# A two-layer diffusion backbone: gate build on one engine, reordered candidate pairs, and early expert blocks in the routing

## The chip, the cores and the metric

The kernel runs on one core of a Trainium2 chip. A core has a matrix engine (TensorE, PE in the profile), a vector engine (VectorE, DVE), a scalar engine (ScalarE, ACT), a general one (GpSimd, POOL) and SyncE (SP), whose queue issues most transfers. Each engine runs its own instructions in their order and waits for others by semaphores. The metric is the device time of one execution in microseconds (us); lower is better.

## What is computed

Two layers over 512 latent tokens and 256 context tokens, 1024 wide. The part of a layer that matters here is its second half, a product-key expert network with 16384 experts:

```python
def _peer(xn, wq, sub_keys, u_tab, v_tab):
    s1, i1 = lax.top_k(s[:, :, 0], 16)          # s: 8 heads, two halves, 128 keys each
    s2, i2 = lax.top_k(s[:, :, 1], 16)
    cand_s = s1[..., :, None] + s2[..., None, :]
    cand_i = i1[..., :, None] * 128 + i2[..., None, :]
    top_s, pos = lax.top_k(cand_s, 16)          # over the 256 pairs
    idx, gate = take(cand_i, pos), softmax(top_s)
    a = gelu(einsum('nd,nhkd->nhk', xb, u_tab[idx])) * gate
    return einsum('nhk,nhkd->nd', a, v_tab[idx])
```

Layer 0 does this for all 768 tokens, layer 1 for the 512 latent ones. All data are float32.

## The kernel before

**Dense and gathered tokens.** For most latent tokens (`DENSE`: 512 in layer 0, 384 in layer 1) the experts are not gathered. Their gates are spread into a matrix G (16384 experts by tokens, mostly zeros), and the network is computed densely, in 128 blocks of 128 experts: `h = gelu(U_c x)`, times G, times `V_c`. The 256 context tokens of layer 0 and the last 128 latent tokens of layer 1 are gathered row by row from a table that holds u and v side by side: a generator (`gather`, L1208) that at every step fetches two table rows of 8 KB for each of 128 tokens (2 MB in all, issued from GpSimd's queue, L1249), and for the rows of earlier steps takes the dot product with x (L1231) and adds the weighted v (L1223), all of that on VectorE. A block of tokens takes 64 steps and three more.

**Stages of the second half**, in this order, with layer 0's place in the profiled execution:

- routing (`route`, L1050; 788 to 1009 us): 16 half-heads. For each, ScalarE and GpSimd split a weight block into a high and a low part (L1075, L1076), TensorE makes the queries with 24 matmuls and the key scores with 4, and VectorE picks the top 16 of 128 for each of four token tiles (L1107 to L1116). After every second head `route_pick` (L1132) runs for each tile as a generator of three pieces: GpSimd adds the pairs of sums and of ids into `rcd` (`CAND`: of the 256 pairs only 50 can hold one of the best 16); VectorE finds the best 8 and the next 8 (L1160 to L1168) and compares their places with an iota (L1172), GpSimd multiplies the one-hot result by the ids (`roh`, L1174); VectorE sums it (L1177).
- gate build (`build_g`, L1308; 1009 to 1295 us): 64 iterations of 8 tokens in layer 0, 48 in layer 1. In each, VectorE makes two one-hot tiles of 128x1024 float16 (`goa`, `gob`, L1353, L1354) and multiplies the first by the gates' high part (`go1`, L1355); the product with the low part (`go2`, L1359) is made by GpSimd, in every third iteration by VectorE. TensorE multiplies them (16 matmuls), ScalarE moves the result to a stage of 2 MB, and every four iterations SyncE writes that to memory (`Gd`).
- dense stage (`dense`, L1396; 1317 to 2615 us): 128 blocks, each with a hidden part (24 matmuls, L1383) and an output part (24 matmuls in layer 0, 18 in layer 1).

**Work put into other stages.** The hidden part of the blocks in `EARLY` (26 of each layer's 128) is computed ahead by the generator `early` (L1389) and written to memory, from where the dense stage loads it. Its split into a low part (`dul`, L1378) is GpSimd's; in the dense stage it is VectorE's. `advance(n)` takes n blocks from that generator: `ROUTE` per half-head (0), `TAIL` (8) behind the routing, 0.2 per iteration of the build, the rest behind the build. Likewise `steps(n)` takes n steps from the gathers: `STEP_BUILD` (0.15 and 0.1) per iteration of the build; what is left is spread evenly over the dense stage (L1470).

**What sets the order.** The program text is not the order on the engines: a scheduler places each instruction where its own model finds it ready, so that a few early blocks of `TAIL` stand between the routing's matmuls. The resulting order on each engine is fixed when the kernel is built.

## Time and profile before

| what | us |
|---|---|
| median of 3 runs | 4478.73 (4469.4 to 4480.89) |
| the profiled execution, its own time | 4476.18 |
| its span, first to last instruction | 4474.4 |
| TensorE busy in it | 3992.0 (89%) |
| VectorE busy | 3283.9 (73%) |
| GpSimd busy | 1705.1 (38%) |
| ScalarE busy | 1571.2 (35%) |

The page gives such shares for the whole span, in which stages with different limits follow each other. So the stretches of the stages have to be read apart: for each, the busy time of every engine, the clock that TensorE was granted as a part of full speed, and the busy share of the 16 transfer engines. A matmul's duration overlaps the next one's; how long one takes in a row of them is read from the distance between starts. The same holds for VectorE, by some 0.07 us.

### The profile page before, as it was taken

How to read it: one execution, taken by the hardware profiler on the slowest of the kernel's cores; microseconds unless marked ns; L12 is line 12 of the kernel's file. 1: busy time of each engine (PE TensorE's matmuls, PEld its weight loads, DVE VectorE, ACT ScalarE, POOL GpSimd, SP SyncE). 2: the span in 40 equal slices, each digit the busy share in tenths (PEclk: the TensorE clock that was granted, in tenths of full speed). 3: DMA queues.
4: the chain of work that ended last, by engine and by line, in shares of the span. 5: the costliest groups of instructions: out<-in, count | busy, mean ns of one | idle time of the engine just before them, and what ended most of it. 6: DMA issues, size and time to landing. Idle time of an engine off the chain costs nothing. (4 is left out here: it accounts for less than half of the span.)

```text
span 4474.4 us, 57073 instructions
## 1 busy us (share of the span) xinstructions
PE 3992.0 (89%) x20829; PEld 3352.4 (75%) x20829; DVE 3283.9 (73%) x6347; ACT 1571.2 (35%) x2562; POOL 1705.1 (38%) x1363
## 2 busy tenths in 40 slices
PE   7889878877869999999999969888868899999998
PEld 4568657666658888777888859677667799999998
DVE  2444686589978888788888755674889577777775
ACT  2332243325543333223323233433246333333332
POOL 2133354785633333233333133345876222222220
PEclk8899889988879999999999989989978899999999
DMA  7663221317779889888889634123257788788875
GB/s 264 226 208 108 60 71 62 112 61 221 227 250 352 332 333 335 322 319 324 338 334 343 247 114 119 50 81 100 65 164 216 265 307 303 294 311 301 301 300 168
DMA packets 429346, 996.46 MB, mean 223 GB/s; under 512 B 31448, under 2 KB 264280, under 8 KB 375816
## 3 DMA queue, kind: packets, MB, share of 16 engines
q1 hardware_dynamic: 372760, 586.46, 38.3%
q0 software_dynamic: 56304, 406.35, 24.4%
q8 instruction: 164, 2.69, 0.2%
q14 instruction: 118, 0.97, 0.1%
HBM read 909.97 MB, written 81.17 MB: 222 GB/s over the span
## 5 line engine op out<-in xcount | busy, mean ns | idle before, releaser
L1249 POOL DMA_INDIRECT uv<-in_peer_uv_dram,ridx x384 | 633.3, 1649 | 1558.2 <-DVE eacc L1223 1506.8
L141 PE MATMUL o<-dvh,dch 128*128 128x512 f32 x1792 | 702.0, 392 | 3.5 <-DVE do L1425 3.5
L141 PE MATMUL o<-dvl,dch 128*128 128x512 f32 x1792 | 701.3, 391 | 0.0
L141 PE MATMUL o<-dvh,dcl 128*128 128x512 f32 x1792 | 697.2, 389 | 0.0
L1383 PE MATMUL h<-xh,duh 128*128 128x512 f32 (+1 forms) x1632 | 602.9, 369 | 47.5 <-ACT duh L1377 39.9
L1383 PE MATMUL h<-xh,dul 128*128 128x512 f32 (+1 forms) x1632 | 604.8, 371 | 0.4 <-DVE dul L1378 0.3
L1383 PE MATMUL h<-xl,duh 128*128 128x512 f32 (+1 forms) x1632 | 602.2, 369 | 0.0
L1223 DVE SCALAR_TENSOR_TENSOR eacc<-uv,egf,eacc 128x1024 f32<-128x1024 f32 x381 | 492.4, 1293 | 0.0
L1231 DVE SCALAR_TENSOR_TENSOR uv<-uv,xn 128x1024 f32<-128x1024 f32 x384 | 470.3, 1225 | 0.0
L1377 ACT CAST duh<-du 128x1024 fp32r<-128x1024 f32 x256 | 268.7, 1050 | 535.4 <-PE h L1383 455.6
L1378 DVE TENSOR_TENSOR dul<-du,duh 128x1024 fp32r<-128x1024 f32 x204 | 249.5, 1224 | 261.9 <-ACT duh L1377 225.6
L141 PEld LDWEIGHTS o<-dvh,dch 128*128 128x128 f32 x1792 | 336.3, 188 | 78.1 <-DVE do L1425 7.2
L141 PEld LDWEIGHTS o<-dvh,dcl 128*128 128x128 f32 x1792 | 336.5, 188 | 73.6 <-DVE dcl L1462 0.3
L141 PEld LDWEIGHTS o<-dvl,dch 128*128 128x128 f32 x1792 | 336.3, 188 | 66.6
L1450 ACT CAST dvh<-dv 128x1024 fp32r<-128x1024 f32 x256 | 263.1, 1051 | 350.1 <-PE o L141 298.0
L1451 DVE TENSOR_TENSOR dvl<-dv,dvh 128x1024 fp32r<-128x1024 f32 x256 | 308.8, 1221 | 101.5 <-ACT dvh L1450 82.1
L1383 PEld LDWEIGHTS h<-xh,duh 128*128 128x128 f32 x1632 | 309.1, 189 | 90.2 <-ACT duh L1377 40.5
L1383 PEld LDWEIGHTS h<-xl,duh 128*128 128x128 f32 x1632 | 309.0, 189 | 42.1
L1383 PEld LDWEIGHTS h<-xh,dul 128*128 128x128 f32 x1632 | 308.6, 189 | 39.1 <-DVE dul L1378 1.9
L141 PE MATMUL mm<-go,gob 128*128 128x128 f16 x1792 | 238.1, 297 | 94.0 <-DVE go L1355 79.0
L141 PEld LDWEIGHTS <-gob 128*128 128x128 f16 x1792 | 194.8, 120 | 141.4 <-DVE go L1355 100.6
L1365 ACT ACTIVATE gst<-mm 128x512 f32<-128x512 f32 x224 | 226.3, 1120 | 166.3 <-PE mm L141 153.6
(352 smaller groups left out, 8027.9 us busy)
## 6 DMA issues: line engine op xcount, KB each, us to landing
du<-in_peer_ut_dram SPq DMA_DIRECT2D x256, 512.0 KB
dv<-in_peer_v_dram SPq DMA_DIRECT2D x256, 512.0 KB
Gd<-gst SPq DMA_DIRECT2D x28, 2048.0 KB
wa<-in_w_ada_dram SPq DMA_DIRECT2D x24, 2048.0 KB
w<-in_w_in_dram SPq DMA_DIRECT2D x78, 512.0 KB
dG<-Gd SPq DMA_DIRECT2D x32, 1024.0 KB
w<-in_peer_wq_dram SPq DMA_DIRECT2D x48, 512.0 KB
dG<-Gd SPq DMA_DIRECT2D x32, 768.0 KB
```

Source lines behind the costliest of these rows:

```text
L141: self.nc.tensor.matmul(out, lhsT=lhsT, rhs=rhs, start=start, stop=stop)
L1223: nc.vector.scalar_tensor_tensor(acc, t[:, D:], w, acc, op0=OP.mult, op1=OP.add)
L1231: nc.vector.scalar_tensor_tensor(t[:, :D], t[:, :D], 1.0, xn, op0=OP.mult, op1=OP.mult, accum_out=dots[:, k:k + 1])
L1249: nc.gpsimd.indirect_dma_start(t, None, a["peer_uv"], bass.IndirectOffsetOnAxis(ap=idx[:, k:k + 1], axis=0))
L1365: nc.scalar.activation(stage[:, :, q * 8 + g * 4:q * 8 + g * 4 + 4].rearrange("p i t -> p t i"), gp.rearrange("p (t i) -> p t i", i=P), AF ...
L1377: nc.scalar.copy(uh, u)
L1378: eng.tensor_sub(ul, u, uh.bitcast(F32))
L1383: nc.tensor.matmul(hp[:, :nd], lhsT=lt[:, k], rhs=rt[:, k, :nd], start=n == 0, stop=n == 3 * KD - 1)
L1450: nc.scalar.copy(vh, v)
L1451: nc.vector.tensor_sub(vl, v, vh.bitcast(F32))
```

## The change

Six things, all in the second half of the layers:

1. In the gate build the product `go2` is VectorE's in every iteration.
2. No gather steps are taken in the build (`steps(STEP_BUILD[l])` is gone); all of them fall to the dense stage.
3. While the build runs, the low part of an early block is made by VectorE instead of GpSimd.
4. `EARLY` has 32 blocks instead of 26, and `ROUTE` is 0.75: 12 blocks are taken within the routing, then 8 behind it and 0.2 per iteration of the build as before.
5. The 50 candidate pairs are reordered so that the 20 that can hold one of the best 8 come first. The first `max` and its `max_index` search those 20. The pairs are added by 12 GpSimd instructions per tile instead of 8.
6. The comparison, the product and the sum that turn places into ids work on 8 picks of 20 and 8 picks of 50 instead of 16 of 50, all three on VectorE and in the generator's third piece.

```diff
-STEP_BUILD = (0.15, 0.1)
-ROUTE = (0, 0)
+ROUTE = (0.75, 0.75)
-EARLY = (tuple(range(1, 128, 5)), tuple(range(1, 128, 5)))
+EARLY = (tuple(range(1, 128, 4)), tuple(range(1, 128, 4)))
-CAND = ((0, 1, 16, 0), (1, 1, 8, 16), (2, 1, 5, 24), (3, 1, 4, 29), (4, 1, 3, 33), (5, 3, 2, 36), (8, 8, 1, 42))
+CAND = ((0, 1, 0, 8, 0), (1, 1, 0, 4, 8), (2, 2, 0, 2, 12), (4, 4, 0, 1, 16),
+        (0, 1, 8, 8, 20), (1, 1, 4, 4, 28), (2, 1, 2, 3, 32), (3, 1, 2, 2, 35), (4, 1, 1, 2, 37), (5, 3, 1, 1, 39),
+        (8, 8, 0, 1, 42))
+NTOP = 20
...
-                    nc.vector.max(v0, ca[:, h])
+                    nc.vector.max(v0, ca[:, h, :NTOP])
...
-        eq = T(pw, [P, NCAND, K], F16, tag="req")
-        nc.vector.tensor_tensor(eq, tf[:, None, :].to_broadcast([P, NCAND, K]), iota, op=OP.is_equal)
-        oh = T(pw, [P, RH, 16, NCAND], tag="roh", bufs=nt // 2)
-        nc.gpsimd.tensor_mul(oh, eq.rearrange("p c (h k) -> p h k c", k=16),
-                             ci[:, :, None, :].to_broadcast([P, RH, 16, NCAND]))
         yield
-        nc.vector.tensor_reduce(ef[:, h0 * 16:(h0 + RH) * 16], oh.rearrange("p h k c -> p (h k) c"), axis=AX.X, op=OP.add)
+        for x, nx in enumerate((NTOP, NCAND)):
+            eq = T(pw, [P, nx, RH * 8], F16, tag=f"req{x}")
+            nc.vector.tensor_tensor(eq, tf[:, x].rearrange("p h k -> p (h k)")[:, None, :].to_broadcast([P, nx, RH * 8]),
+                                    iota[:, :nx], op=OP.is_equal)
+            oh = T(pw, [P, RH, 8, nx], tag=f"roh{x}")
+            nc.vector.tensor_mul(oh, eq.rearrange("p c (h k) -> p h k c", k=8),
+                                 ci[:, :, None, :nx].to_broadcast([P, RH, 8, nx]))
+            nc.vector.tensor_reduce(e4[:, :, x], oh, axis=AX.X, op=OP.add)
...
-                n += 1
+                nc.vector.tensor_tensor(o2, oa, bc(e16[3]), op=OP.mult)
                 self.advance(0.2)
-                self.steps(STEP_BUILD[l])
-                (nc.vector if n % 3 == 0 else nc.gpsimd).tensor_tensor(o2, oa, bc(e16[3]), op=OP.mult)
...
-            ge = self.hidden(l, c, pool, pool, xh, xl, "sm", self.nc.gpsimd)
+            ge = self.hidden(l, c, pool, pool, xh, xl, "sm", self.nc.vector if self.building else self.nc.gpsimd)
```

The order on the engines moves with it. On VectorE in layer 0's gate build, before (`go` stands for both products; L1359 is `go2`, here the third iteration's, and `uv`, `eacc` are a gather's):

```order
L1353 TENSOR_TENSOR goa_9524<-e_1789_8623,iota_1788_8621 128x1024
L1354 TENSOR_TENSOR gob_9525<-e_1790_8624,iota_1788_8621 128x1024
L1355 TENSOR_TENSOR go_2001_9526<-goa_9524,e_1791_8625 128x1024
L1359 TENSOR_TENSOR go_2002_9527<-goa_9524,e_1792_8626 128x1024
L1353 TENSOR_TENSOR goa_9554<-e_1789_8623,iota_1788_8621 128x1024
L1354 TENSOR_TENSOR gob_9555<-e_1790_8624,iota_1788_8621 128x1024
L1355 TENSOR_TENSOR go_2008_9556<-goa_9554,e_1791_8625 128x1024
L1223 SCALAR_TENSOR_TENSOR eacc_8864<-uv_9080,egf_9320,eacc_8864 128x1024
L1231 SCALAR_TENSOR_TENSOR uv_9323,dots_8863<-uv_9323,xn_4947 128x1024
L1231 SCALAR_TENSOR_TENSOR uv_9325,dots_8863<-uv_9325,xn_4947 128x1024
L1353 TENSOR_TENSOR goa_9627<-e_1789_8623,iota_1788_8621 128x1024
```

The same place after the change (L1362 to L1365 are the four operations of an iteration, L1385 is `dul`):

```order
L1362 TENSOR_TENSOR goa_10164<-e_1909_9259,iota_1908_9257 128x1024
L1363 TENSOR_TENSOR gob_10165<-e_1910_9260,iota_1908_9257 128x1024
L1364 TENSOR_TENSOR go_2118_10166<-goa_10164,e_1911_9261 128x1024
L1365 TENSOR_TENSOR go_2119_10167<-goa_10164,e_1912_9262 128x1024
L1385 TENSOR_TENSOR dul_10175<-du_10172,duh_10174 128x1024
L1362 TENSOR_TENSOR goa_10226<-e_1909_9259,iota_1908_9257 128x1024
L1363 TENSOR_TENSOR gob_10227<-e_1910_9260,iota_1908_9257 128x1024
L1364 TENSOR_TENSOR go_2129_10228<-goa_10226,e_1911_9261 128x1024
L1365 TENSOR_TENSOR go_2130_10229<-goa_10226,e_1912_9262 128x1024
```

The gather's rows are gone from the build, every iteration has four VectorE operations, and an early block's subtraction comes now and then. On TensorE, 12 early blocks stand in layer 0's build (15 before) and 11 in layer 1's (12 before).

On TensorE in layer 0's routing, before: the last two matmuls of an early block (`sm`) that stand behind a half-head's queries, the half-head's key scores, and the next half-head's queries:

```order
L1383 MATMUL sm_8477<-xh_6640,duh_8473 128x512
L1383 MATMUL sm_8477<-xl_6641,duh_8473 128x512
L141 MATMUL mm_7583<-keysT_7487,qt_7581 128x128 x4
L141 MATMUL mm_7619<-xh_6640,wh_7552 128x512
L141 MATMUL mm_7619<-xl_6641,wh_7552 128x512
L141 MATMUL mm_7619<-xh_6640,wl_7553 128x512
```

and after:

```order
L1390 MATMUL sm_7963<-xh_6724,duh_7959 128x512
L145 MATMUL mm_7921<-keysT_7791,qt_7919 128x128 x4
L1390 MATMUL sm_7963<-xl_6725,duh_7959 128x512
L1390 MATMUL sm_7963<-xh_6724,dul_7960 128x512
...
L1390 MATMUL sm_7963<-xl_6725,duh_7959 128x512
L1390 MATMUL sm_7963<-xh_6724,dul_7960 128x512
L145 MATMUL mm_7991<-xh_6724,wh_7856 128x512
L145 MATMUL mm_7991<-xl_6725,wh_7856 128x512
```

Before, 7 matmuls of an early block stand between a half-head's queries and its scores, and none behind the scores. After, 17 more of them stand behind the scores; so it is in six of the half-heads, and in four others 8 or 10. Counted over layer 0's routing, 20 early blocks stand ahead of the build instead of 11, and 7.8 of them (188 matmuls) behind the last key scores instead of 4.8 (116 matmuls); in layer 1 it is 19.1 instead of 13.8 blocks, and 162 instead of 146 matmuls behind the last scores.

On GpSimd in layer 0's routing, before (`wl` is a weight block's low part, `dul` an early block's, `roh` the product with the ids):

```order
L1149 TENSOR_TENSOR rcd_7770<-rsf_1486_6812 128x2x6
L1146 TENSOR_TENSOR rcd_7770<-rsf_1486_6812 128x4x8
L1076 TENSOR_TENSOR wl_7921<-w_7918,wh_7920 128x1024
L1174 TENSOR_TENSOR roh_8157<-req_8155,rcd_7737 128x1600
L1174 TENSOR_TENSOR roh_8175<-req_8173,rcd_7748 128x1600
L1076 TENSOR_TENSOR wl_7984<-w_7981,wh_7983 128x1024
L1174 TENSOR_TENSOR roh_8193<-req_8191,rcd_7759 128x1600
L1378 TENSOR_TENSOR dul_8576<-du_8573,duh_8575 128x1024
L1174 TENSOR_TENSOR roh_8211<-req_8209,rcd_7770 128x1600
```

and after:

```order
L1151 TENSOR_TENSOR rcd_7722<-rsf_1514_6896 128x4x3
L1151 TENSOR_TENSOR rcd_7722<-rsf_1514_6896 128x4x8
L1080 TENSOR_TENSOR wl_7857<-w_7854,wh_7856 128x1024
L1385 TENSOR_TENSOR dul_8055<-du_8052,duh_8054 128x1024
L1080 TENSOR_TENSOR wl_7954<-w_7951,wh_7953 128x1024
L1385 TENSOR_TENSOR dul_8369<-du_8366,duh_8368 128x1024
L1080 TENSOR_TENSOR wl_8049<-w_8046,wh_8048 128x1024
```

The products with the ids are gone; the subtractions of weights and of early blocks take turns.

## Rows read from the trace of the kernel before

**Rows 1.** From the page: busy time, share of the span and instructions of each engine.

```profile
PE 3992.0 (89%) x20829; PEld 3352.4 (75%) x20829; DVE 3283.9 (73%) x6347; ACT 1571.2 (35%) x2562; POOL 1705.1 (38%) x1363
```

**Rows 2.** Stretches: us, busy PE, PEld, DVE, ACT, POOL, clock, transfer share, GB/s.

```profile
788.00:1009.00 221.00, 181.09 (x777) 143.76 (x777) 161.33 (x826) 65.73 (x130) 173.21 (x177) 0.91 0.27 84
1009.00:1317.00 308.00, 226.83 (x1395) 182.61 (x1395) 273.38 (x292) 157.03 (x185) 171.29 (x79) 0.84 0.71 228
1317.00:2615.00 1298.00, 1283.41 (x5520) 1039.87 (x5520) 1090.60 (x1465) 386.10 (x578) 394.71 (x246) 0.99 0.84 317
3060.00:3285.00 225.00, 182.84 (x863) 157.59 (x864) 162.94 (x833) 72.69 (x143) 180.89 (x183) 0.90 0.29 89
3285.00:3501.00 216.00, 159.78 (x1070) 140.67 (x1069) 189.99 (x191) 117.36 (x138) 121.77 (x54) 0.83 0.69 216
3501.00:4474.40 973.40, 961.29 (x4750) 866.87 (x4750) 702.17 (x928) 350.20 (x519) 199.55 (x121) 0.99 0.77 285
```

**Rows 3.** Timeline of VectorE in layer 0's build: start, us, what.

```profile
1226.42 0.68 DVE L1359 TENSOR_TENSOR go<-goa,e 128x1024 f16<-128x1024 f16 x1
1227.02 0.68 DVE L1354 TENSOR_TENSOR gob<-e,iota 128x1024 f16<-128x1024 f16 x1
...
1228.23 2.88 DVE L1353 TENSOR_TENSOR goa<-e,iota 128x1024 f16<-128x1024 f16 x1
...
1231.63 2.38 DVE L1355 TENSOR_TENSOR go<-goa,e 128x1024 f16<-128x1024 f16 x1
```

**Rows 4.** Timeline of GpSimd in the same microseconds.

```profile
1227.63 2.93 POOL L1378 TENSOR_TENSOR dul<-du,duh 128x1024 fp32r<-128x1024 f32 x1 [1.68 <-issue]
1231.25 2.21 POOL L1359 TENSOR_TENSOR go<-goa,e 128x1024 f16<-128x1024 f16 x1 [0.69 <-DVE goa L1353]
```

**Rows 5.** Groups of instructions of the whole span: busy us, mean ns of one.

```profile
L1355 DVE TENSOR_TENSOR go<-goa,e 128x1024 f16<-128x1024 f16 x112 | 175.0, 1562 | 0.0
L1359 POOL TENSOR_TENSOR go<-goa,e 128x1024 f16<-128x1024 f16 x75 | 173.8, 2322 | 134.6 <-DVE goa L1353 104.0 <-PE mm L141 24.4 <-DVE e L1344 3.7
L1223 DVE SCALAR_TENSOR_TENSOR eacc<-uv,egf,eacc 128x1024 f32<-128x1024 f32 x381 | 492.4, 1293 | 0.0
L1231 DVE SCALAR_TENSOR_TENSOR uv<-uv,xn 128x1024 f32<-128x1024 f32 x384 | 470.3, 1225 | 0.0
L1174 POOL TENSOR_TENSOR roh<-req,rcd 128x1600 f32<-128x1600 f16 x40 | 180.8, 4527 | 32.7 <-DVE req L1172 18.7 <-DVE ref L1177 14.0
L1177 DVE TENSOR_REDUCE ref<-roh 128x32 f32<-128x1600 f32 x40 | 72.4, 1813 | 45.0 <-POOL roh L1174 45.0
```

**Rows 6.** Timeline of TensorE in layer 0's build: an iteration's 16 matmuls, what follows.

```profile
1162.15 2.06 PE L141 MATMUL mm<-go,gob 128*128 128x128 f16 x16 [0.62 <-DVE go L1355]
1163.97 0.48 PE L1383 MATMUL sm<-xl,duh 128*128 128x512 f32 x1
```

**Rows 7.** The write of a stage: last of layer 0 (SyncE's waits), last of layer 1 (chain).

```profile
SPq L199 <- DMA Gd<-gst: 13.3, 1, 13.3
...
3482.57 8.70 DMA Gd<-gst
```

**Rows 8.** TensorE's last key scores and the build's first transposes, layer 0, layer 1.

```profile
958.56 1.16 PE L141 MATMUL mm<-keysT,qt 128*128 128x128 f32 x8 [2.23 <-ACT qt L1096]
1009.06 0.66 PE L196 MATMUL tr<-ident,gif 128*128 128x128 f32 x2 [3.88 <-issue]
...
3235.95 1.16 PE L141 MATMUL mm<-keysT,qt 128*128 128x128 f32 x8 [1.44 <-ACT qt L1096]
3286.99 0.33 PE L196 MATMUL tr<-ident,gif 128*128 128x128 f32 x1 [0.61 <-ACT gsg L1342]
```

**Rows 9.** Layer 0's dense stage: transfer queues, packets, MB, share; a block of layer 1.

```profile
q0 software_dynamic: 33973, 246.42, 50.6%
q1 hardware_dynamic: 42481, 164.08, 33.4%
...
3624.76 4.24 PE h L1383 x24
```

More of the change, by code (lines that the diff above doesn't have):

```diff
@@ L100, in __init__ @@
         self.hold = False
+        self.building = False
     def pool(self, st, name, bufs=1, space=None, side=None):
@@ L1060, in route @@
             self.load(ic, a["iota"][:, :NCAND])
-            iota = self.T(pk, [P, NCAND, RH * 16], F16, tag="iota")
-            nc.vector.tensor_copy(iota, ic[:, :, None].to_broadcast([P, NCAND, RH * 16]))
+            iota = self.T(pk, [P, NCAND, RH * 8], F16, tag="iota")
+            nc.vector.tensor_copy(iota, ic[:, :, None].to_broadcast([P, NCAND, RH * 8]))
             sf = [self.T(pk, [P, 2, 2, NH, 16], tag=f"rsf{i}") for i in range(nt)]
@@ L1140, in route_pick @@
         cd = T(pw, [P, 2, RH, NCAND], tag="rcd", bufs=2 * nt)
-        for a0, na, nb, off in CAND:
+        for a0, na, b0, nb, off in CAND:
             o = cd[:, :, :, off:off + na * nb]
+            sb = sf[:, :, 1, hs, b0:b0 + nb]
             if na == 1:
-                nc.gpsimd.tensor_add(o, sf[:, :, 0, hs, a0:a0 + 1].to_broadcast([P, 2, RH, nb]), sf[:, :, 1, hs, :nb])
+                nc.gpsimd.tensor_add(o, sf[:, :, 0, hs, a0:a0 + 1].to_broadcast([P, 2, RH, nb]), sb)
             elif nb == 1:
-                nc.gpsimd.tensor_add(o, sf[:, :, 0, hs, a0:a0 + na], sf[:, :, 1, hs, 0:1].to_broadcast([P, 2, RH, na]))
+                nc.gpsimd.tensor_add(o, sf[:, :, 0, hs, a0:a0 + na], sb.to_broadcast([P, 2, RH, na]))
             else:
@@ L1150, in route_pick @@
                                          sf[:, q, 0, hs, a0:a0 + na, None].to_broadcast([P, RH, na, nb]),
-                                         sf[:, q, 1, hs, None, :nb].to_broadcast([P, RH, na, nb]))
+                                         sf[:, q, 1, hs, None, b0:b0 + nb].to_broadcast([P, RH, na, nb]))
         ca, ci = cd[:, 0], cd[:, 1]
@@ L1163, in route_pick @@
                 elif fn == 2:
-                    nc.vector.max_index(ti[:, h, 0:8], v0, ca[:, h])
+                    nc.vector.max_index(ti[:, h, 0:8], v0, ca[:, h, :NTOP])
                 elif fn == 3:
@@ L1168, in route_pick @@
                     nc.vector.max_index(ti[:, h, 8:16], v1, wk[:, h])
-        tf = T(pw, [P, K], F16, tag="rtf")
-        nc.scalar.copy(tf, ti.rearrange("p h k -> p (h k)"))
-        eq = T(pw, [P, NCAND, K], F16, tag="req")
-        nc.vector.tensor_tensor(eq, tf[:, None, :].to_broadcast([P, NCAND, K]), iota, op=OP.is_equal)
-        oh = T(pw, [P, RH, 16, NCAND], tag="roh", bufs=nt // 2)
-        nc.gpsimd.tensor_mul(oh, eq.rearrange("p c (h k) -> p h k c", k=16),
-                             ci[:, :, None, :].to_broadcast([P, RH, 16, NCAND]))
-        yield
-        nc.vector.tensor_reduce(ef[:, h0 * 16:(h0 + RH) * 16], oh.rearrange("p h k c -> p (h k) c"), axis=AX.X, op=OP.add)
+        tf = T(pw, [P, 2, RH, 8], F16, tag="rtf")
+        nc.scalar.copy(tf.rearrange("p x h k -> p h x k"), ti.rearrange("p h (x k) -> p h x k", k=8))
+        yield
+        e4 = ef[:, h0 * 16:(h0 + RH) * 16].rearrange("p (h x k) -> p h x k", x=2, k=8)
+        for x, nx in enumerate((NTOP, NCAND)):
[6 more added lines that the diff above has]
+            nc.vector.tensor_reduce(e4[:, :, x], oh, axis=AX.X, op=OP.add)
     def route_gates(self, l, seg, i, pr, pw, ts, ef):
@@ L1294, in peer_lat @@
             self.todo = len(self.bg) * (HK // 2 + 3)
+            self.building = True
             with ExitStack() as s1:
                 self.build_g(s1, l, r)
+            self.building = False
             run(self.bg2 or ())
@@ L1344, in build_g @@
                     nc.vector.tensor_sub(e16[3][:, ts], sg[:, :m], e16[2][:, ts])
-        n = 0
         for tb in range(nd // TB):
```

## The prediction

> **What bounds the kernel now.** The page's first part gives TensorE 89% of the span [rows 1], which says little, for the span is a chain of stages. So I read it by stretches [rows 2]. In the two dense stages TensorE is busy in 1283 of 1298 us and 961 of 973: there it is the bound, and nothing but fewer matmuls helps. In the gate builds it is not (227 of 308, 160 of 216, at a granted clock of 0.84): VectorE is, with 273 of 308 and 190 of 216. In the two routings no engine is full: TensorE 181 of 221 and 183 of 225, GpSimd 173 and 181, VectorE 161 and 163. There the engines hand work round in turn.
>
> Next, why VectorE is full in the build. Its timeline shows two sorts of the same 128x1024 float16 operation: 0.68 us, at a distance of 0.60 to the next, and 2.38 or 2.88 us [rows 3]. GpSimd's timeline beside it [rows 4] tells them apart: a VectorE operation that starts at 1228.23 ends at 1231.11, 0.55 after GpSimd's subtraction ends (1230.56); one that starts at 1231.63 ends at 1234.01, 0.55 after GpSimd's product (1233.46). So the slow form is an operation that waits until GpSimd has finished and then takes its usual time. The mean of `go1` is 1.56 us for that reason, and GpSimd's `go2` takes 2.32 each time [rows 5].
>
> **The change part by part.** The sum is made against the profiled execution's own time, 4476.2 (span 4474.4); the median of the runs is 2.5 higher.
>
> *Build, layer 0.* VectorE after: 64 iterations of four operations at 0.60, 154 us, and 12 subtractions of early blocks at 1.22 (the mean of a 128x1024 float32 operation with two inputs, as L1231 in [rows 5]), 15: 169. The nine gather steps that left took two rows a step, 2 x (1.29 + 1.23) = 5.0 us each [rows 5], 45 in all. GpSimd computes nothing there any more, so the slow form has nobody to wait for. TensorE after: 16 matmuls of an iteration take 1.82 (1162.15 to 1163.97, [rows 6]), 64 x 1.82 = 116; an early block's 24 matmuls at the dense stage's pace (1298 / 5520 = 0.235 us, [rows 2]) 5.6, and 12 of them stand there: 68. Together 184. Writes of the stage: 16, between 8.7 us each (alone) and 13.3 (with other transfers under way) [rows 7]: 139 to 213. I take 8.7, since the gathers that ran beside them are gone; 213 stays as a rival. So TensorE becomes the bound at 184, with VectorE close to it; engines that hand work to each other at such loads don't reach 100%, and I put 5% for it, the loss between none and 15%: 194. What of the stretch VectorE did not fill (308 - 273 = 35: setting up, and the last write with the reloads behind it) stays. 194 + 35 = 229 for 308: **-79** (-89 to -60).
>
> *Build, layer 1.* In the same way: VectorE 48 x 2.4 + 11 x 1.22 = 129; TensorE 48 x 1.82 + 11 x 4.24 (a block of 384 tokens, [rows 9]) = 134; writes 12 x 8.7 = 104. 134 with 5% is 141, and 216 - 190 = 26 stay: 167 for 216: **-49** (-56 to -36).
>
> *Routing, layer 0.* GpSimd loses 16 products `roh` of 4.53 us [rows 5], 72 of its 173 busy us, and gets 9 more subtractions of early blocks (2.93 us, [rows 4]), 26, and four more small adds per tile, for which no row stands here but ample room: it is far from full then. VectorE gets the products: 1120 elements a tile, at the reduction's 1.13 ns each (1813 / 1600, [rows 5]) 1.3 us, and saves a third of the reduction, 0.5: 0.8 a tile, 13 us more on 161, less what it no longer waits for GpSimd. The block seen in [rows 3, 4] can come back here, since these operations too stand beside GpSimd's subtractions. The Trainium skill (SBUF — State Buffer, Who interferes with whom) says between which: a VectorE instruction with two SBUF inputs and a GpSimd one that reads SBUF, the second to start waiting for the whole of the first. By that rule the 9 new subtractions could add up to 26 us to VectorE, which the sum leaves out, since VectorE has room for them; they would lean towards rival D. TensorE gets 9 more blocks, 9 x 5.64 = 51 us, for which it has 40 idle ones [rows 2]. Behind the last key scores, where 50 us passed (958.6 to 1009.1, [rows 8]) while GpSimd and VectorE finished the ids, 188 matmuls now stand, 44 us. If every idle microsecond were used the build would start 11 later; if none, 51. With GpSimd's long products gone most are: **+15** (0 to +51).
>
> *Routing, layer 1.* 5.3 more blocks at 4.24 are 22 us, for 42 idle ones. Behind the last scores 51 us passed [rows 8]; the 162 matmuls there take 29, and the chain of ids without `roh` about 35. **-10** (-20 to +22).
>
> *Dense, layer 0.* Six blocks less: 6 x 5.64 = 34 us on the bound. Against it, VectorE gets the nine steps (45) and loses six subtractions (7): 1091 + 38 = 1129 of 1264, 89% for 84%. The transfers: 246 MB of gathers took 50.6% of 1298 us [rows 9], 2.67 us per MB; nine steps are 19 MB, 50 us, and the share goes from 0.84 to 0.90. Before, TensorE lost 15 us there. I put 15 more for the double steps that now fall into some blocks, between 0 and the whole 45: **-19** (-34 to +11).
>
> *Dense, layer 1.* 6 x 4.24 = 25 less; four steps more, 20 us, on a VectorE that is 72% busy and transfers at 0.77: hidden, but for 3. **-22** (-25 to -5).
>
> *The rest.* The loads and stores of six more early blocks (SyncE's queue) replace as many in the dense stage. In layer 0 the context's routing runs beside attention on a TensorE with other work: its eight `roh` on GpSimd are worth 0 (-8 to +3).
>
> Sum: -79 - 49 + 15 - 10 - 19 - 22 = -164, so 4312 in the profile and **4315** as a median.
>
> **The rivals.**
>
> *A, slower: the slow form stays.* If the 2.4 us are not GpSimd's doing, `go2` costs VectorE what `go1` costs, 1.56 on the mean, and nothing else in the build gets shorter. Layer 0: 273 - 45 (gathers) - 14 (the 21 `go2` it had) + 64 x 1.56 + 15 = 329, so +56; layer 1: 190 - 20 - 11 + 75 + 13 = 247, +57. With the other terms (+5, -41): 4476 + 77, about **4556** with the 2.5. It decides from 0.87 us per `go2`: below that, what leaves the build and the dense stage pays for it. For it: VectorE is the full engine, and 75 operations go onto it. Against it: the ends of [rows 3] follow those of [rows 4] by the same 0.55 both times. 4%.
>
> *A', the same with `go2` at 0.60.* Then the builds keep their length but for 45 + 28 on VectorE and 65 off it, +8, and the sum is +8 + 5 - 41: **4451**. 3%. The Trainium skill (Perfetto Trace Analysis, Optimizing Scalar/DVE Operations) speaks for this case: a saturated VectorE should rather give work away, to GpSimd even; the same section doubts it between these two, which share a read port, and rows 3 and 4 bear out the doubt.
>
> *B, the writes bound the builds.* At 13.3 each: 213 for 194, 160 for 141, +38: **4353**. For it: a stage has two buffers, and four iterations now take 12 us. Against: 8.7 where nothing else ran. 12%.
>
> *C, the dense stages take the steps back.* All of 45 and 20 us of moved VectorE work exposed: +47: **4362**. For it: two resources near 90%. Against: before, at 84%, TensorE lost 15 of 1298. 12%.
>
> *D, the routing shows the added blocks in full* (TensorE's order is fixed; whenever it waits for scores, nothing else fills in): +51 and +22 instead of +15 and -10: **4383**. 8%.
>
> *E, no loss at any of these places:* builds at 184 and 134 (-89, -56), routing 0 and -20, dense -34 and -25: -224, about **4255**. 9%.
>
> That the change doesn't do what it says is excluded by the order: the four operations of an iteration stand on VectorE, the gathers are gone from the build, and 20 blocks stand ahead of it.
>
> **How the numbers follow.** The forecast (4280 to 4345) has 52%, A 4%, A' 3%, B and C 12% each, D 8%, E 9%. The range takes in B to E and leaves out A and A': 4245 to 4395. About 0.3% (13 us) can be told from no change. Faster by more than that: all but A, less a little for mixtures, 0.94; within it 0.02; slower 0.04.
>
> **What would show it.** In the build: no VectorE operation of 128x1024 float16 over 1 us, iterations of 2.8 to 3.2 us, layer 0's build stretch near 229 and layer 1's near 167, TensorE's clock above 0.84. In the routing: the first build transposes some 15 us later in layer 0, no later in layer 1. In the dense stages: TensorE idle below 30 us, and layer 0's gathers landing in time. It is wrong if slow operations remain in the build without GpSimd work beside them (A), if ScalarE waits for a stage's write (B), or if TensorE's idle time in the dense stage grows by more than 30 (C).

## The result and the profile after

The changed kernel took **4423.28 us** (median of 4 runs, 4407.88 to 4425.21) beside 4479.81 for the kernel before: ratio 0.9869 [0.9841, 0.9898]. That is 57 us less, where 164 were forecast, and less than the range allowed. The profiled execution took 4424.53, its span is 4422.8.

From the page of the changed kernel, the engines' busy time (it answers [rows 1]):

```profile
PE 3990.4 (90%) x20829; PEld 3362.6 (76%) x20829; DVE 3228.7 (73%) x6592; ACT 1568.2 (35%) x2562; POOL 1339.3 (30%) x1398
```

GpSimd lost a fifth of its work, TensorE and VectorE next to none: where the time went has to be seen by stretch. The six stretches of [rows 2] in the changed kernel, cut at the same events (routing, build, dense stage; layer 0, then layer 1; the columns are those of [rows 2]):

```profile
775.70:1052.00 276.30, 234.22 (x993) 187.61 (x993) 201.73 (x893) 80.12 (x149) 137.98 (x239) 0.91 0.31 101
1052.00:1271.00 219.00, 195.14 (x1325) 165.06 (x1323) 172.72 (x282) 152.34 (x170) 0.00 (x0) 0.92 0.73 224
1271.00:2579.00 1308.00, 1264.32 (x5376) 1021.12 (x5376) 1114.95 (x1516) 374.48 (x575) 416.39 (x261) 0.98 0.86 325
3029.50:3292.00 262.50, 205.06 (x979) 181.09 (x980) 195.02 (x895) 77.20 (x148) 125.96 (x232) 0.87 0.28 88
3292.00:3474.80 182.80, 157.66 (x1088) 144.53 (x1086) 133.10 (x213) 116.45 (x136) 16.93 (x8) 0.89 0.75 235
3474.80:4422.80 948.00, 935.96 (x4608) 841.22 (x4608) 705.86 (x941) 342.71 (x510) 206.20 (x125) 0.99 0.79 295
```

Layer 0's build fell from 308 to 219 with GpSimd at 0.00; its routing rose from 221 to 276; its dense stage, with 144 matmuls fewer, rose from 1295 (without the idle end that [rows 2] includes) to 1308, and TensorE's idle time there from 12 to 44. By these stretches, which are those of the forecast, the builds got 89 and 33 us shorter and the routings 55 and 38 longer.

VectorE in layer 0's build, where [rows 3] had 0.68 beside 2.88 and 2.38 (start, us, what):

```profile
1150.83 0.69 DVE L1364 TENSOR_TENSOR go<-goa,e 128x1024 f16<-128x1024 f16 x1
1151.44 0.69 DVE L1365 TENSOR_TENSOR go<-goa,e 128x1024 f16<-128x1024 f16 x1
1152.04 0.69 DVE L1362 TENSOR_TENSOR goa<-e,iota 128x1024 f16<-128x1024 f16 x1
1152.64 0.69 DVE L1363 TENSOR_TENSOR gob<-e,iota 128x1024 f16<-128x1024 f16 x1
```

Only one form is left, all 256 operations of the stage between 0.68 and 0.70. That step of the argument was right.

To follow the rest through the experiments, every traced kernel is cut at the same starts on TensorE: first early block (`sm`), last key scores, first and last gate matmul (`go`), first dense matmul (`h`), first transposes of the next layer. Microseconds between them:

```
                     to first   layer 0                                    be-    layer 1
                     block   route  tail  build   end   dense  tween  route  tail  build   end  dense   span
before                789.2  169.4  60.8  274.3  23.8  1313.4  432.7  172.3  55.0  190.1  19.0  974.4  4474.4
after                 775.7  220.2  62.8  191.8  20.4  1326.6  431.9  216.4  59.4  149.2  20.3  948.0  4422.8
e1 rtf buffers        771.0  209.5  65.5  193.5  20.2  1333.9  434.8  215.4  60.5  149.2  20.4  947.8  4421.5
e2 old picks          786.6  203.3  68.7  191.8  19.1  1323.0  432.0  204.0  72.2  152.0  19.4  948.5  4420.6
e3 no added blocks    768.3  179.6  50.9  194.1  40.0  1328.2  433.6  187.1  52.1  148.6  38.2  971.0  4391.7
e4 build only         779.3  169.4  52.8  191.7  41.8  1337.8  432.9  171.7  50.1  148.4  39.6  971.0  4386.6
e5 steps in build     767.9  215.9  67.1  227.7  22.1  1335.4  430.1  213.9  60.8  154.6  21.6  948.5  4465.6
e6 blocks in tail     770.2  187.9  62.0  195.2  19.5  1328.0  433.5  195.0  64.2  144.9  19.3  972.8  4392.5
e7 e6 + du            771.5  188.1  62.0  195.2  19.5  1307.8  433.1  195.1  65.2  145.4  19.3  973.7  4376.0
e8 after + du         772.4  217.3  64.4  190.8  20.3  1281.6  434.8  213.7  59.1  149.2  20.1  947.8  4371.7
e9 e4 + tail + du     788.3  169.1  65.6  194.6  19.4  1307.8  433.6  176.4  72.6  141.2  19.3  974.4  4362.3
e10 e3 + tail + du    779.3  179.6  56.2  195.8  19.6  1313.5  434.8  187.2  65.0  144.0  19.0  973.6  4367.6
e11 before + du       781.1  169.6  61.1  275.3  23.9  1304.3  433.7  174.5  57.1  190.3  19.5  974.3  4464.6
e12 e9, 32 blocks     787.0  170.3  93.3  196.1  20.7  1285.7  431.2  172.4  81.0  150.7  23.0  948.2  4359.8
e13 e10, roh GpSimd   771.3  196.2  62.7  194.4  20.1  1309.4  430.2  195.4  68.6  145.0  18.3  974.1  4385.7
```

By these cuts the builds with their ends gave 86 and 40, layer 1's dense stage 26, the stretch ahead of layer 0's first block 13.5; the routings with their tails took 53 and 48, layer 0's dense stage 13. Together that is the 52 us between the spans. (In layer 1 these cuts show 6 us more gained in the builds and 11 more lost in the routings than the stretches above, mainly because a build's stretch begins with its first transposes, 13 us ahead of the first gate matmul after the change and 4 before.)

### The profile page after: what moved, and what is told of

The parts are those of the page before. It is cut to its first block, busy times and chain, and to the rows that moved or that the text cites. A ratio compares the mean times of both kernels' runs of the same rounds, so it can differ in the third digit from the quotient of the medians.

```text
span 4422.8 us, 57298 instructions
## 1 busy us (share of the span) xinstructions
PE 3990.4 (90%) x20829; PEld 3362.6 (76%) x20829; DVE 3228.7 (73%) x6592; ACT 1568.2 (35%) x2562; POOL 1339.3 (30%) x1398
## 5 line engine op out<-in xcount | busy, mean ns | idle before, releaser
L1390 PE MATMUL h<-xh,duh 128*128 128x512 f32 (+1 forms) x1536 | 570.9, 372 | 63.4 <-ACT duh L1384 32.5
L1390 PE MATMUL h<-xh,dul 128*128 128x512 f32 (+1 forms) x1536 | 571.0, 372 | 1.3 <-DVE dul L1385 1.2
L1390 PE MATMUL h<-xl,duh 128*128 128x512 f32 (+1 forms) x1536 | 568.9, 370 | 0.0
L1385 DVE TENSOR_TENSOR dul<-du,duh 128x1024 fp32r<-128x1024 f32 x214 | 261.4, 1222 | 246.6 <-ACT duh L1384 227.5
L1390 PEld LDWEIGHTS h<-xh,duh 128*128 128x128 f32 x1536 | 292.1, 190 | 106.8 <-ACT dge L1393 35.6
L1390 PEld LDWEIGHTS h<-xl,duh 128*128 128x128 f32 x1536 | 292.2, 190 | 39.7
L1390 PEld LDWEIGHTS h<-xh,dul 128*128 128x128 f32 x1536 | 291.3, 190 | 39.6 <-DVE dul L1385 4.2
L1468 ACT CAST dch<-dcf 128x512 fp32r<-128x512 f32 (+1 forms) x256 | 145.2, 567 | 310.9 <-DVE dcf L1465 299.9
```

Of the source, the lines that this page charges most:

```text
L1385: eng.tensor_sub(ul, u, uh.bitcast(F32))
L1390: nc.tensor.matmul(hp[:, :nd], lhsT=lt[:, k], rhs=rt[:, k, :nd], start=n == 0, stop=n == 3 * KD - 1)
L1468: m1 = nc.scalar.copy(ch, cf)
```

## The experiments

**First: which part does what?** Four kernels. e1 gives the cast `rtf` more buffers; e2 undoes the change of the picks; e3 undoes the added early blocks; e4 is the kernel before with parts 1 to 3 alone.

```diff
e1, in the changed kernel
-        tf = T(pw, [P, 2, RH, 8], F16, tag="rtf")
+        tf = T(pw, [P, 2, RH, 8], F16, tag="rtf", bufs=nt)
e2: the changed kernel with CAND, route_pick and its iota as before
e3, in the changed kernel
-ROUTE = (0.75, 0.75)
-EARLY = (tuple(range(1, 128, 4)), tuple(range(1, 128, 4)))
+ROUTE = (0, 0)
+EARLY = (tuple(range(1, 128, 5)), tuple(range(1, 128, 5)))
e4: the kernel before with the diff's hunks on build_g, STEP_BUILD and self.building
```

> The changed kernel with four buffers for the places as float16 (rtf) instead of two. Read in the trace of the changed kernel: ScalarE's cast rtf waits for VectorE's comparison req 58 us in layer 0's routing (8 times, up to 11.3) and 34 in layer 1's, because req now stands a piece later and holds the buffer; queued behind it on ScalarE are the cast of the next weights (wh) and the copy of the queries (qt) for which TensorE's key scores wait. Theory 1 (that buffer): these waits vanish, and of TensorE's waits for key scores in layer 0 (31 us) the three that follow an rtf (8.1, 7.1, 7.7) go, so layer 0's routing gets some 15 to 23 us shorter; in layer 1 the three long ones (12.8, 12.6, 10.4) follow the cast rsf, so little goes there: about 4403. Theory 2 (VectorE has more to do, which was 41 us more in layer 0's routing and 32 in layer 1's, and ScalarE would wait for something else of VectorE's at the same moment): no gain, 4423 within 6. Theory 3 (the added early blocks show in full on TensorE because its order is fixed): no gain either.

> The changed kernel with parts 5 and 6 undone: candidate pairs, searches and the product roh on GpSimd as in the kernel before; build and early blocks as changed. Theory 2 (the picks' product on VectorE lengthens the routing): layer 0's routing 276 to about 250, layer 1's 262 to about 235, so about 4370. Theory 1 (the rtf buffer): the comparison is again in the same piece as the cast, so its waits go as in the run with four buffers, about 4400. Theory 3 (the added early blocks show in full): routing stays within 6 us, or gets longer by GpSimd's 72 us of products, 4420 to 4460.

> The changed kernel with part 4 undone: 26 early blocks a layer and none taken within the routing; picks and build as changed. Theory 3 (added blocks show in full, 9 of 5.6 us in layer 0 and 5 of 4.2 in layer 1): the routings come back to 225 and 240 us; the dense stages get six blocks more each, 34 and 25 us. If besides the 47 us that layer 0's dense stage lost per block count came of the closer spacing of early blocks there (every fourth), they go too: about 4380; if they came of the moved gather steps, about 4415. Theories 1 and 2 (rtf's buffer, VectorE): the routings stay above 245 and 250, and the time rises to about 4440.

> The kernel before with parts 1 to 3 alone: the build's second product on VectorE, no gather steps in the build, the low parts of early blocks on VectorE while the build runs. The builds get 121 us shorter, as they did in the changed kernel (89 and 32). What is asked is what the dense stages give back for nine and four more gather steps: if the loss in layer 0's dense stage is due to these steps, about 45 us, 4480 - 121 + 45 = 4404; if it is due to the early blocks standing every fourth instead of every fifth, they cost about 5, and the time is 4365. The routings stay at 220 and 223.

Measured, beside 4474.92 for before: e1 4411.85, ratio 0.9856 [0.9837, 0.9875] (it can't be told from the changed kernel); e2 4424.93, 0.9899 [0.9875, 0.9922]; e3 4394.29, 0.9832 [0.9809, 0.9854]; e4 4391.08, 0.9816 [0.9799, 0.9833]. So parts 1 to 3 alone are worth 84 us, more than the whole change. The picks (parts 5, 6) are worth nothing that can be told from noise either way: 3 us from e4 to e3, -2 from e2 to the changed kernel. The added early blocks cost 29 to 34 (e3 to the changed kernel, e4 to e2; 31 and 34 by the spans). The second of these is clear of the noise by itself, the first isn't: the intervals of e3 and of the changed kernel overlap. Without the added blocks e3's routings with their tails are back at 231 and 239, as theory 3 said.

Where they cost: the stretch from the first block to the last key scores, e4, then e2, in layer 0:

```profile
779.30:948.70 169.40, 148.42 (x653) 118.83 (x653) 125.09 (x695) 52.92 (x105) 133.38 (x135) 0.93 0.29 88
```

```profile
786.60:990.00 203.40, 182.01 (x797) 147.19 (x797) 148.84 (x696) 61.94 (x117) 149.90 (x141) 0.94 0.30 95
```

144 matmuls more are six blocks, 34 us longer, and TensorE's idle time is 21 us in both. The added blocks found none of it: theory 3 holds in layer 0. In layer 1 4.5 blocks (18 us of busy time) took 32, so idle time grew too: TensorE waited 9.1 us three times there for the copy of a half-head's queries, the first time here:

```profile
3105.78 2.07 PE L141 MATMUL mm<-keysT,qt 128*128 128x128 f32 x8 [9.12 <-ACT qt L1096]
```

Each time 15 matmuls of added blocks stand ahead of these queries' own matmuls and only put them off.

e1's theory fell in its main part. ScalarE's and TensorE's waits in layer 0's routing (who waited for whom: us in total, times, longest), first of the changed kernel:

```profile
ACT rtf L1175 <- DVE req L1180: 58.3, 8, 11.3
...
PE mm L145 <- ACT qt L1100: 31.4, 6, 8.1
...
ACT rsf L1142 <- DVE riv L1120: 24.4, 4, 8.8
```

and of e1:

```profile
ACT rsf L1142 <- DVE riv L1120: 43.9, 4, 16.5
...
PE mm L145 <- ACT qt L1100: 29.2, 5, 9.8
ACT rtf L1175 <- DVE rti L1173: 28.4, 16, 5.1
```

The wait for `req`, 58 us, is gone. Of it 36 came back: `rtf` waits 28 instead of 13 for the searches that it reads (`rti`), and `rsf`, the next cast on ScalarE, which needs VectorE's searches too, 44 instead of 24; TensorE waits 29 us for its queries instead of 31. Layer 0's routing got 11 shorter, layer 1's 1.

**Second: what holds the dense stage, and can blocks be had free in the tail?** e5 takes the gather steps back into the build; e6 is e3 with e1's buffers and more blocks given out behind the routing; e7 and e8 add a third buffer for `du`, the load of a block's part of U (512 KB), in the dense stages to e6 and to the changed kernel.

```diff
e5, in the changed kernel's build_g
+STEP_BUILD = (0.15, 0.1)
...
+                self.steps(STEP_BUILD[l])
e6, in e3 with e1's edit
-TAIL = (8, 8)
+TAIL = (13, 16)
e7 = e6, e8 = the changed kernel, both with
-        u = self.T(pu, [P, KD, P], tag="du", bufs=2)
+        u = self.T(pu, [P, KD, P], tag="du", bufs=3 if tag == "h" else 2)
```

> The changed kernel with part 2 undone: the gather steps are again taken in the gate build (0.15 and 0.1 an iteration), all else as changed. With the build-only kernel, layer 0's dense stage took 1338 us for 1313 before with the same 102 blocks: 24 us for the moved steps. The changed kernel has six blocks less and took 1327, 47 more than its count of blocks asks for. Theory D1 (the moved steps, alone): its dense stage falls to about 1280. Theory D2 (the early blocks at every fourth place, whose TensorE work is half and whose gather and load work is not, have a part of their own): it falls to about 1303. In both the builds take the steps back, VectorE 166 + 42 of layer 0's 190, so some 20 to 35 us longer in layer 0 and 5 to 10 in layer 1: by D1 about 4405, by D2 about 4430.

> The kernel without the added early blocks (26 a layer, none taken within the routing; picks and build as changed), with four buffers for rtf, and with 13 (layer 0) and 16 (layer 1) early blocks instead of 8 given out behind the routing. On TensorE 7.5 and 9.2 blocks then stand between the last key scores and the first gate matmul, for 2.8 and 1.5, and 0.2 and none behind the build, for 5.2 and 7.8. Theory: early blocks are free where TensorE is idle and nothing else can fill it (27 of 51 us there in layer 0, 39 of 52 in layer 1), and cost in full where they stand among the key scores: the stretch behind the last key scores stays within 8 us, the end of the build gets 19 and 20 us shorter, rtf's buffers give some 8: about 4348. Rival (they show in full here too, as the casts on ScalarE and the subtractions on GpSimd that make a block hold the chain of the picks): 26 and 33 us longer there, about 4400.

> The kernel before this one in the list, with three buffers instead of two for the block of down-weights (du) in the dense stages. In the changed kernel ScalarE waited 95 us for this load in layer 0's dense stage (19 before), and the load is issued when VectorE's subtraction of the block before last sets its buffer free, which now stands behind more gather work. Theory D3 (lateness of that load, for want of a buffer): layer 0's dense stage, 1328 without the buffer, falls by 15 to 24 us. Rival D4 (VectorE, busy in 85% of the stage, itself hands its products over late): it falls by less than 6.

> The changed kernel with three buffers instead of two for du in the dense stages, and nothing else changed. Theory D3: layer 0's dense stage falls from 1327 to about 1290 (up to 47 less) and the time to about 4388. Rival D4: 4420 within 6.

Measured, beside 4475.36: e5 4475.46, ratio 0.9995 [0.9982, 1.0009]; e6 4398.21, 0.9830 [0.9809, 0.9851]; e7 4381.66, 0.9792 [0.9771, 0.9813]; e8 4371.42, 0.9767 [0.9741, 0.9792].

e8 settles the dense stage. Layer 0's, changed kernel, then e8:

```profile
1271.10:2597.70 1326.60, 1264.33 (x5377) 1021.16 (x5378) 1123.11 (x1538) 379.07 (x582) 418.01 (x264) 0.98 0.86 324
```

```profile
1265.20:2546.80 1281.60, 1252.00 (x5377) 1011.46 (x5377) 1122.46 (x1538) 379.39 (x582) 415.83 (x264) 0.99 0.88 336
```

45 us less with the same instructions on every engine, and 1281.6 is what the forecast's pace gives for six blocks less (1313.4 - 33.8 = 1279.6). How the loss came about is seen at one of its gaps in the changed kernel; ScalarE, VectorE, SyncE and TensorE, one timeline each:

```profile
1516.28 1.04 ACT L1384 CAST duh<-du 128x1024 fp32r<-128x1024 f32 x1 [10.77 <-DMA du<-in_peer_ut_dram]
1517.23 0.59 ACT L1393 ACTIVATE dge<-h 128x512 f32<-128x512 f32 x1
```

```profile
1500.50 1.28 DVE L1231 SCALAR_TENSOR_TENSOR eacc<-uv,egf,eacc 128x1024 f32<-128x1024 f32 x1
...
1505.18 1.23 DVE L1385 TENSOR_TENSOR dul<-du,duh 128x1024 fp32r<-128x1024 f32 x1
...
1517.36 1.22 DVE L1385 TENSOR_TENSOR dul<-du,duh 128x1024 fp32r<-128x1024 f32 x1 [9.14 <-ACT duh L1384]
```

```profile
1506.44 2.18 SPq L203 DMA_DIRECT2D du<-in_peer_ut_dram  x2
```

```profile
1517.87 0.80 PE L1390 MATMUL h<-xh,duh 128*128 128x512 f32 x1 [4.62 <-ACT dge L1393]
...
1562.06 0.50 PE L1390 MATMUL h<-xh,duh 128*128 128x512 f32 x1 [2.31 <-ACT dge L1393]
...
1610.63 0.79 PE L1390 MATMUL h<-xh,duh 128*128 128x512 f32 x1 [4.62 <-ACT dge L1393]
```

A `du` buffer is set free by `dul` on VectorE, which stands behind a gather's rows (1500.5 to 1505.2). Only then, at 1506.4, does SyncE issue the next load; the data are there at 1516.3, and ScalarE and VectorE have waited 10.8 and 9.1. TensorE waits 4.6, by the profile for `dge`, the gelu of the block before; its input was ready at 1511.9, but on ScalarE it stands behind the cast that waits for `du`. The gaps lie 44 to 49 us apart: four blocks, the spacing of the early ones, at each of which TensorE does half a block's matmuls; that it therefore wants the next `du` sooner is argued from this spacing. ScalarE's waits for this load in the stage, of the changed kernel:

```profile
ACT duh L1384 <- DMA du<-in_peer_ut_dram: 94.8, 12, 10.8
```

Before there were 3 of them, 18.7 us; in e8, as in every kernel here with a third buffer, 0.2 us of one are left. With three buffers a load no longer needs the buffer of the block just ahead of it.

In e5, with the steps back in the build, the stage still took 1335.4, so the steps can't be the only cause: theory D1 fell, and D2's size too. e4, with moved steps and the old spacing, lost 24. Either alone delays the loads: ScalarE waited 59.8 us for them in e4, and in e5

```profile
ACT duh L1386 <- DMA du<-in_peer_ut_dram: 136.9, 15, 11.3
```

e7, at the old spacing, got 20 back. What e5 did show is the price of the steps in the build: 38 us there in layer 0 and 7 in layer 1, and with them the whole change is worth nothing.

e6 gave nothing against e3. In the tails 4.7 and 7.7 blocks more (27 and 33 us of TensorE) did cost only 11 and 12, and the ends got 21 and 19 shorter, but the routings got 8 us longer each, where the `rtf` buffers had been expected to give some 8. The same blocks stand in them as in e3; the four `rtf` buffers are the only other edit.

**Third: do the findings add up?** e9 is e4 with more blocks in the tail and the third buffer; e10 the same with the new picks, two `rtf` buffers; e11 the kernel before with the buffer alone; e12 is e9 with 32 blocks and none within the routing.

```diff
e9 = e4, e10 = e3, both with du's third buffer and
-TAIL = (8, 8)
+TAIL = (13, 16)
e11 = the kernel before with du's third buffer
e12, in e9
-TAIL = (13, 16)
-EARLY = (tuple(range(1, 128, 5)), tuple(range(1, 128, 5)))
+TAIL = (18, 18)
+EARLY = (tuple(range(1, 128, 4)), tuple(range(1, 128, 4)))
```

> The build-only kernel (parts 1 to 3 of the change; picks and 26 early blocks as before) with 13 and 16 early blocks given out behind the routing instead of 8, and a third buffer for du in the dense stages. If the two findings so far add up: layer 0's dense stage 1338 to about 1313, the stretch behind the last key scores some 10 us longer in each layer and the end of each build some 22 shorter, the routings at 170 and 172 as there: 4391 - 24 - 20, about 4347. If the third buffer only mended what the early blocks at every fourth place had broken, the dense stage stays near 1335 and the time near 4370.

> The kernel before this one in the list with parts 5 and 6 (picks on VectorE) added; it is also the kernel with four rtf buffers, blocks in the tail and a third du buffer, with two rtf buffers again. Theory P (the picks' work on VectorE, 42 us more of it in layer 0's routing than before, lengthens the routings by 10 and 15 us while the stage before them gets some 10 shorter): 10 to 18 slower than the kernel before it in the list, with routings of 180 and 187. Theory 1, as far as it stands (two rtf buffers hold ScalarE): routings not shorter than with four, 188 and 195, about 4382. By the kernels without added early blocks it should be the other way: with two buffers 180 and 187, so about 4362.

> The kernel before with a third buffer for du in the dense stages and nothing else. Its ScalarE waited 19 us for that load in layer 0's dense stage and TensorE stood idle there for 11 us in four gaps. So at most 11 to 15 us: about 4464 to 4470. If more comes, the buffer does something else than meet late loads, and the reading of the other runs with it falls.

> The first kernel of this list with 32 early blocks a layer instead of 26 (every fourth) and 18 given out behind each routing, none of them within it: 12.5 and 11.2 blocks stand behind the last key scores, 1.2 and 3.8 behind the build. Theory (a block costs in full wherever TensorE has no idle time left, and is paid back in full by the dense stage if du has its third buffer): 34 and 25 us less in the dense stages, 28 and 9 more behind the key scores, 6 and 16 more behind the builds: the same time within 8 us. Rival (early blocks at every fourth place cost the dense stage something of their own, third buffer or not): 20 to 40 slower.

Measured, beside 4477.86: e9 4363.02, ratio 0.9738 [0.9721, 0.9755]; e10 4359.78, 0.9735 [0.9718, 0.9751]; e11 4465.98, 0.9974 [0.9964, 0.9983]; e12 4358.94, 0.9732 [0.9715, 0.9748]. Three kernels, equal by their intervals, are some 60 us faster than the changed kernel.

e11 gives the 12 us that the waits allowed, no more. e9's dense stage came as expected (1307.8 for 1313), 3.5 above e11's: with the third buffer the moved gather steps cost that little. e9's tails cost more than in e6 (13 and 22 for 3.7 and 7.7 blocks), hence 4363 for 4347. e10 against e7 speaks against four `rtf` buffers once more: routings of 180 and 187 for 188 and 195. Beside e9 its routings are 10 and 11 longer, as theory P said, but it is not 10 to 18 slower: the stage ahead is 9 shorter and the tails 9 and 8, so the picks cost nothing on the whole here either. e12 is the clean test of place, against e9. Layer 0 from the first block to the last scores, and from there to the first gate matmul, in e9:

```profile
788.30:957.40 169.10, 147.65 (x653) 118.53 (x653) 125.04 (x695) 53.36 (x105) 133.44 (x135) 0.93 0.29 88
957.40:1023.10 65.70, 50.06 (x201) 38.92 (x202) 45.25 (x152) 19.91 (x43) 47.25 (x48) 0.84 0.38 130
```

and in e12:

```profile
787.00:957.30 170.30, 147.12 (x654) 118.08 (x654) 127.17 (x695) 53.22 (x105) 133.33 (x135) 0.93 0.29 87
957.30:1050.60 93.30, 77.40 (x320) 60.62 (x321) 45.33 (x152) 27.58 (x53) 59.35 (x53) 0.91 0.49 176
```

Five blocks more (119 matmuls) cost 27.6 us, 27.3 of them busy: in full, and the 16 us in which TensorE stays idle there are the same in both. From e4 to e9 the first 3.7 blocks had still used some: 22 us more of busy time for 13. The dense stages pay 22 and 26 back (1307.8 to 1285.7, 974.4 to 948.2), the first of them less than the theory's 34; the tail, build and end of layer 1 take some of that, and the sum is nil within 8 us, as the theory said.

**Last: why do the new picks lengthen the routing?** From e4 to e3 it got 10 and 15 us longer. e13 is e10 with the product back on GpSimd, with the two buffers that it had there before, and the comparison back in the piece of the search.

```diff
e13, in e10's route_pick (the comparison and this product stand ahead of the yield)
-            nc.vector.tensor_mul(oh, eq.rearrange("p c (h k) -> p h k c", k=8),
+            nc.gpsimd.tensor_mul(oh, eq.rearrange("p c (h k) -> p h k c", k=8),
```

> The kernel with new picks, 13 and 16 early blocks behind the routing and a third du buffer, but the products with the ids (roh) back on GpSimd and the comparison back in the piece of the search, as in the kernel before; the ordered candidates and the halved work (8 picks of 20 and 8 of 50) stay. So of the picks' change only the move of the product from GpSimd to VectorE is undone. Theory P (that move costs the routing: the product's 42 us on VectorE, part of it spent waiting for GpSimd's subtractions): routings 180 and 187 fall to about 170 and 174, and to the 4363 and 4360 of the kernels with old and with new picks stands about 4350. Rival (the routings are longer with the new picks because there are twice as many comparisons, products and sums per tile): they stay at 180 and 187, the time at 4360 or above.

Measured: 4394.26 beside 4474.86, ratio 0.9832 [0.9818, 0.9845]; the routings 196 and 195. Theory P fell: undoing the move made it worse. Waits of TensorE, ScalarE and GpSimd in e13's layer 0, routing and tail:

```profile
PE mm L145 <- ACT qt L1100: 40.1, 5, 12.9
ACT rsf L1142 <- DVE riv L1120: 38.5, 4, 16.8
...
POOL roh L1183 <- DVE ref L1188: 16.4, 7, 5.7
```

The wait is at the same cast again. The rival, that twice as many small operations are the cause, isn't shown either, since in e13 GpSimd also waited 16 us for the buffers of its products (the last line). What lengthens the routing with the new picks is left open; the place where it shows is ScalarE's cast `rsf` ahead of the queries' copy.

## Why the prediction was wrong, step by step

- **Builds: right in layer 0, short in layer 1.** By the stretches of the forecast -89 and -33 (forecast -79 and -49, the second with a range of -56 to -36); with their ends, by the table, -86 and -40. TensorE was the bound as forecast, and in layer 0 nearer to full than the 5% put for losses: 189.1 of 191.8 us. Writes (rival B) bound nothing; ScalarE never waited for one. In layer 1 1.8 early blocks stand behind the build, and TensorE was busy in only 137.3 of 149.2.
- **Routing: the failed step.** Forecast +15 and -10, measured +53 and +48 with the tails. The sum let the added blocks use idle TensorE time because there was as much of it. Idle time in a fixed order belongs to a place: the added blocks stand ahead of a half-head's query matmuls, the wait comes behind these, for ScalarE's copy, and there as many early matmuls stand as before (7, by the order shown ahead of the prediction). From the first block to the last scores TensorE's idle time didn't fall but rose, from 21 to 34 us in layer 0. Behind the last scores some of it was used (2.9 blocks more, the tail 2 us longer). Rival D, at 8%, had the mechanism: there the blocks cost 34 and 32 by e4 and e2, in full in layer 0 and in layer 1 more than in full, which D's +22 doesn't cover. For layer 1 the forecast also let the stretch behind the last scores shrink from 51 to about 35; it didn't get shorter (55.0 to 59.4).
- **Picks in the routing: mis-sized.** 0.8 us a tile more on VectorE were put down, 13 in all, and hidden. The comparison, product and sum took 33.4 + 42.3 + 23.1 = 99 us in the changed kernel, 76 in e3 and 57 before. The product was put at 1.13 ns an element, 20 us for 16 tiles of 1120; in e3 it took 37.6, or 2.1 ns. The 23 between e3 and the changed kernel come with the added early blocks, whose subtractions are GpSimd's; with the old picks it is 20 (e4 to e2). The sum had left out such a slowing, which rests on [rows 3, 4], because VectorE had room; but its searches stand on the chain to `rsf`. Beside the added blocks (e2 to the changed kernel) the picks cost 17 and 12 us of routing and made the tails 6 and 13 shorter.
- **Picks, the stage before: missed.** Forecast 0 (-8 to +3). The eight kernels with new picks on VectorE reach the first early block after 768 to 779 us, the six with old ones, before among them, after 779 to 789; the means are 772 and 785. That gain is about half of what the picks cost in the routings (10 and 15, e4 to e3). The product's move from GpSimd doesn't seem to make it: e13, with the product back there, reaches that block after 771. What does is open.
- **Dense, layer 0: the second failed term.** -19 forecast, +13 measured: 47 us lost where 15 were put. That is rival C's price of 45, but not its cause, so the agreement is luck. C was argued from VectorE and the transfers near 90%; e8 has VectorE at 88% and transfers at 0.88 and loses nothing. It was the two `du` buffers. The reading that in the dense stages only fewer matmuls help was wrong too: the third buffer alone gave the kernel before 9 us there (e11). What would have shown it is ScalarE's wait for `du` in the trace before (18.7 us), with the question of which VectorE instruction releases that load.
- **Dense, layer 1: right** (-26 for -22).

The Trainium skill (SBUF — State Buffer, Who interferes with whom) was weighed in the prediction with up to 26 us for nine more subtractions. The 23 us above are of that size, so the trace agrees in size; that each microsecond of them is such a wait isn't shown. In one place of the changed kernel's layer 0, VectorE, then GpSimd:

```profile
841.38 3.39 DVE L1180 TENSOR_TENSOR req<-rtf,iota 128x320 f16<-128x320 f16 x1
...
850.00 0.57 DVE L1180 TENSOR_TENSOR req<-rtf,iota 128x800 f16<-128x800 f16 x1
```

```profile
839.85 2.40 POOL L1080 TENSOR_TENSOR wl<-w,wh 128x1024 fp32r<-128x1024 f32 x1
842.21 2.38 POOL L1385 TENSOR_TENSOR dul<-du,duh 128x1024 fp32r<-128x1024 f32 x1
```

The first comparison, 0.30 us at its shortest, ends 0.18 after GpSimd's second subtraction, though that one began 0.8 after it: here VectorE stood through the rest of one subtraction and the whole of the next. The second comparison, behind 5 us of searches and a product, ends at 850.57 and frees `rtf`. So the slow form is some 3 of the 11.3 us that ScalarE waits here:

```profile
850.66 0.22 ACT L1175 CAST rtf<-rti 128x32 f16<-128x32 uint32 x1 [11.30 <-DVE req L1180]
850.78 1.04 ACT L1079 CAST wh<-w 128x1024 fp32r<-128x1024 f32 x1
851.73 0.58 ACT L1100 COPY qt<-mm 128x512 f32<-128x512 f32 x1
```

TensorE had finished these queries at 842.7 and waited 8.07 us for `qt`, though the copy has nothing to do with `rtf`. The Trainium skill (PSUM — Partial Sum Buffer, Engine vs sequencer instructions) calls ScalarE's queue strictly first in, first out; these rows agree.

## What to carry to other kernels

Idle time of an engine with a fixed order is a set of gaps at places: before work is added to fill it, count what the order puts into each gap, for what stood elsewhere cost its full time here, or more. When steps are moved onto an engine, ask which of its later instructions set buffers free and which loads wait for them; a third buffer was worth 45 us of layer 0's dense stage where the engine's load said nothing. And take a change of several parts apart: here three parts together were worth 84 us, one cost some 30 and two were worth nothing.

## What the runs showed of the hardware

Up to layer 0's first early block, 780 us, kernels with the same work there differed by up to 10 us from one traced execution to another (e4 779.3, before 789.2); a stage's difference of that size needs more than one trace. Of a wait of 58 us taken from one instruction of ScalarE, 36 came back: 16 at the same cast, for its other input, and 20 at the next one. In three of the changed kernel's comparisons (3.4 us each) VectorE stood through two GpSimd subtractions that followed each other, and not only through the one under way when they began.
